# Split operands for the state products of a state space layer, and three moved loads, in a two-layer encoder

## The chip, the cores and the metric

The kernel runs on one core of a Trainium2 chip. A core has five engines that work side by side, each with its own in-order queue: PE (the matrix engine), DVE (vector work), ACT (scalar functions, casts), POOL and SP. SP computes nothing here; it issues most DMA transfers. An engine's queue stalls as a whole when the instruction at its head waits for a semaphore. The metric is the device time of one launch in microseconds (us); lower is better.

## What is computed

The reference is an encoder of two layers over 512 tokens of width 1024, in float32. Each layer is a token mixer and then a gated channel mixer (up-projection, convolution of width 3, gelu, down-projection), with RMS norms before and after each. The first mixer is retention plus neighbourhood attention. The second is a state space layer in both directions, and its chunked scan is where most of the change lies:

```python
def step(h, inp):                     # one chunk of 128 tokens
    qq, kk, vv, aa = inp
    cs = jnp.cumsum(aa, axis=1)
    ...
    y_inter = jnp.einsum('bjgn,bghnp->bjghp', qq, h) * jnp.exp(cs)[..., None]
    tail = jnp.exp(cs[:, -1:] - cs)
    h_new = h * jnp.exp(cs[:, -1])[..., None, None] \
          + jnp.einsum('blgn,blghp->bghnp', kk, vv * tail[..., None])
    return h_new, y_intra + y_inter
```

The last `einsum` is the state product: 128 state channels by 512 inner channels of a group, summed over the 128 tokens of a chunk. There are 4 groups, 4 chunks and 2 directions; the state after the last chunk is not needed, so 3 products are made for each group and direction, 24 in all.

## The kernel before

Tokens lie in 4 chunks of 128. Weights arrive as tiles of 128 by 1024 (512 KB) in `wst`, a staging pool of 3 buffers. `Env.wunit` (L61) issues the load on SP and has `Env.split` (L83) make two operands of it: ACT casts the tile to the reduced type `R32` (`whi`, L86), DVE subtracts that from the original (`wlo`, L87). `Env.mm3` (L89) then takes three products of split operands, high by high, low by high and high by low (L91, L92, L93). All the large projections are made this way. The small products of the mixers take plain F32 operands, one `matmul` call each.

No order is written out for the engines. The program is written as a sequence, a scheduler places each instruction in its engine's queue by its own idea of when it can run, and `high_priority` (L70) lets the weight splits go ahead. A change in one place can so move its neighbours.

The parts of the program, in order of time, with the names that matter here:

- `trunk` (L943) loads the four token tiles of x on SP, with the first norm's gain (`bcast`, L78, a row of 4 KB copied to all 128 partitions) after the first of them and a weight tile after each of the others. `E.norm` (L132) squares a tile of x on ACT (L128), takes the root on POOL (L121) and scales on DVE (`xs`, L139); `E.turn` (L143) transposes it on PE (`pt`, L148) and splits it (`xh`, `xl`).
- `mixer0`, then the first `ffn` (L224).
- `mixer1` (L563), the state space layer. It goes through its 4 groups by a table of steps, `SLOTS` (L551). Step `s` calls `state` (L725) for both directions: DVE scales a chunk of the input (`xs`, L730), PE makes the product with `bt`, the transposed B of the group (`st`, L732), and DVE adds it to the decayed state before (L738, L740), or ACT copies it for the first chunk (L735). Step `i` reads the states (`pi`, L783). Step `h` makes the decays of a head with 8 small ACT instructions on `pb` (L762), a DVE copy (L764), an exponential into `e` (L766) and a product (L768); `e` comes from the pool `m1e` of 5 buffers. Step `p` uses them (`py`, L803).
- At the end of `mixer1`, the output projection of the last group; `out_tile` reloads a half row of x from DRAM after each use of its buffer (L869, `x<-xd`, 8 loads on SP).
- the second `ffn`. It begins with the splits of its first four weight tiles (`w0`, L251): two go to `whi` and `wlo`, two to free buffers of its own, `hh` and `hl`.

Of the kernel before, what the change touches and what calls it, by code (L numbers as in the profile page):

```python
# [7 lines left out]
F32 = mybir.dt.float32  # L8
# [18 lines left out]
class Env:  # L27
# [32 lines left out]

    def wunit(self, src, parts=None):  # L61


        nc = self.nc
        st = self.wst.tile([P, 1024], F32, name="wst")
        nc.sync.dma_start(st, src)
        halves = slice(0, 512), slice(512, 1024)
# [9 lines left out]

    def bcast(self, row):  # L78

        g = self.gain.tile([P, D], F32, name="gain")  # L80
        self.nc.sync.dma_start(g, row.partition_broadcast(P))
        return g
# [139 lines left out]

def ffn(E, w_up, cw, w_down, g_post_row, done):

    nc, tc = E.nc, E.tc
    with ExitStack() as ctx:
        hp = ctx.enter_context(tc.tile_pool(name="ffn_h", bufs=NF))
        cp = ctx.enter_context(tc.tile_pool(name="ffn_c", bufs=1))
        cwt = cp.tile([P, 2, NF, 4], F32, name="cwt")
        nc.sync.dma_start(cwt, cw)  # L230
        hs = []
# [18 lines left out]
        extra = lambda i=0: [hp.tile([P, S], R32, name=n) for n in ("hh", "hh", "hl", "hl")]  # L250
        w0 = [[E.wunit(w_up[s, f], extra() if 2 * f + s >= 2 else None) for s in range(2)] for f in range(2)]  # L251
        p0 = [[E.mm.tile([P, S], F32, name="mm") for s in range(2)] for f in range(2)]
# [309 lines left out]

def mixer1(E, w_dt, w_fm, cw, dtc, cols, mask, w_out, g_post_row, done):  # L563

# [6 lines left out]
    with ExitStack() as ctx:  # L571
# [100 lines left out]

        def to_tok(src, dst):
            pt = E.px.tile([P, NT, P], F32, name="pt", tag="px")
            for c in range(NT):
                nc.tensor.transpose(pt[:, c], src[:, c * C:(c + 1) * C], E.ident)  # L676
            nc.scalar.copy(dst, pt)

# [20 lines left out]
        def silus(o):  # L699
# [6 lines left out]
            for r, _, i in o["silu"]:  # L706
                o["t"][i] = r
                if i == 0:
                    o["bt"] = one.tile([P, NT, P], F32, name="bt")
                    to_tok(r, o["bt"])  # L710
                elif 2 <= i < 6:
                    if "x" not in o:
                        o["x"] = two.tile([P, NT, 512], F32, name="xt")
                    to_tok(r, o["x"][:, :, (i - 2) * P:(i - 1) * P])
            o["silu"] = []
# [9 lines left out]
        def state(o, dr, i):  # L725
# [3 lines left out]
            xs = E.tmp.tile([P, 512], F32, name="xs", tag="tmp")  # L729
            nc.vector.tensor_tensor(hv(xs), hv(o["x"][:, c]), rows(1, dr, g, c), op=ALU.mult)  # L730
            ps = E.px.tile([P, 512], F32, name="st", tag="px")
            nc.tensor.matmul(ps, o["bt"][:, c], xs, start=True, stop=True)  # L732
            ns = one.tile([P, 512], F32, name=f"state{dr}{i}")
# [158 lines left out]
        steps()  # L892
        three, ys, last = pool("m1e", 5), pool("m1y", 2), pool("m1f", 1)
        for _ in range(3):
# [33 lines left out]
        def fin(t, n, m):  # L928
# [3 lines left out]
        ws = [E.wunit(w_out[NG - 1, 0, 0]) + E.wunit(w_out[NG - 1, 0, 1]),  # L932
              E.wunit(w_out[NG - 1, 1, 0], t4(one, ("state00", "state10", "state01", "state11"))) + E.wunit(w_out[NG - 1, 1, 1], t4(four, ("yh", "yh", "yl", "yl")))]
        first = [out_mm(gs[-1], 0, ws[n]) for n in range(2)]
        rms(gs[-1])
# [7 lines left out]
def trunk(tc, x, norms, ab, ssd, ffns, out):  # L943

    nc = tc.nc
    with ExitStack() as ctx:
        E = Env(ctx, tc)
        w0 = []
        for t in range(NT):
            nc.sync.dma_start(E.x[:, t, :], x[t * P:(t + 1) * P])  # L950
            if t == 0:
                g0 = E.bcast(norms[0, 0])
            else:
                w0.append(E.wunit(ab[0][0, len(w0)]))
# [20 lines left out]
        ffn(E, *ffns[0], norms[0, 3], then(norms[1, 0]))  # L975
        mixer1(E, *ssd, norms[1, 1], then(norms[1, 2]))
        ffn(E, *ffns[1], norms[1, 3], store)
        while E.late:
# [108 lines left out]
```

## Time and profile before

| | us |
|---|---|
| median of 3 runs (1420.84 to 1422.39) | 1422.07 |
| the profiled execution, its own time | 1422.91 |
| its span, first to last instruction | 1421.1 |
| PE busy | 1395.8 (98%) |
| DVE busy | 909.3 (64%) |
| ACT busy | 710.6 (50%) |
| start to the first transposition on PE | 8.17 |
| `mixer1` from its first state step to its last | about 700 to 1026 |

Busy times of PE are modelled and overlap from one matmul to the next, so they don't say alone how near PE is to its limit; the distance from one matmul's start to the next does. The profile's clock is the share of the full PE clock that was granted. Times on the axis count from the start of the span.

### The profile page before, as it was taken

The page shows a single profiled execution, that of the slowest core. Times are in us where ns is not written, and L with a number is a line of the kernel's source. Part 1 is how long each engine was busy: PE and PEld are TensorE (multiplying, and loading weights), DVE is VectorE, ACT ScalarE, POOL GpSimd, SP SyncE. Part 2 cuts the span into 40 slices and gives each one's busy share as a digit, 9 for nine tenths or more (in the row PEclk, how much of TensorE's full clock was granted, in tenths as well). Part 3 has the DMA queues.
Part 4 walks back from the last instruction along what each step waited for, and adds up shares of the span by engine and source line. Part 5 has one row for each costly group of instructions (what it writes and reads, how often), then busy time and mean ns, then how long its engine had stood idle before and what let it go on. Part 6 is the DMA issues. An engine that isn't in the chain of part 4 may idle for free.

```text
span 1421.1 us, 17833 instructions
## 1 busy us (share of the span) xinstructions
PE 1395.8 (98%) x6838; PEld 1141.2 (80%) x6838; DVE 909.3 (64%) x1345; ACT 710.6 (50%) x1194; POOL 60.9 (4%) x66
## 2 busy tenths in 40 slices
PE   7999999999999999999999999999989999999998
PEld 6877777898888888888788788787878888888886
DVE  7368888765656652347878686997785665664232
ACT  5346666444444432324878787487344444443230
POOL 1010110100000000000000000010110000000000
PEclk9999999999999999999999999999999999999999
DMA  7443232233233322323566464363342233333231
GB/s 284 150 132 104 85 89 80 77 108 104 89 104 91 102 89 93 129 106 106 140 183 182 148 184 143 101 190 112 124 144 74 91 102 91 102 96 98 89 104 60
DMA packets 56437, 166.33 MB, mean 117 GB/s; under 512 B 6689, under 2 KB 7457, under 8 KB 56353
## 3 DMA queue, kind: packets, MB, share of 16 engines
q1 hardware_dynamic: 48464, 149.99, 33.2%
q10 hardware_dynamic: 7888, 15.21, 3.9%
q8 instruction: 54, 0.88, 0.3%
q14 instruction: 31, 0.25, 0.1%
HBM read 157.57 MB, written 5.51 MB: 115 GB/s over the span
## 4 chain that ended last, share of the span: by engine, by line
PE 89%; DVE 4%; ACT 3%; issue 2%; DMA 1%; POOL 0%; DVEq 0%; SPq 0%; POOLq 0%; ACTq 0%
PE mm L91 27%; PE mm L92 27%; PE mm L93 27%; PE pi L783 2%; PE py L803 1%; PE st L732 1%; PE y L459 1%; PE pt L148 1%; PE sc L443 1%; DVE wlo L87 1%; PE pt L676 0%; PE sc L444 0%; ACT whi L86 0%; DMA x<-in_x 0%; PE pt L511 0%
## 5 line engine op out<-in xcount | busy, mean ns | idle before, releaser
L91 PE MATMUL mm<-xh,whi 128*128 128x512 f32 (+1 forms) x1216 | 463.9, 382 | 0.4 <-ACT xh L86 0.2
L93 PE MATMUL mm<-xl,whi 128*128 128x512 f32 (+2 forms) x1216 | 463.3, 381 | 0.0
L92 PE MATMUL mm<-xh,wlo 128*128 128x512 f32 (+2 forms) x1216 | 462.1, 380 | 0.0
L87 DVE TENSOR_TENSOR wlo<-wst,whi 128x1024 fp32r<-128x1024 f32 (+1 forms) x208 | 254.8, 1226 | 135.0 <-ACT whi L86 131.7
L86 ACT CAST whi<-wst 128x1024 fp32r<-128x1024 f32 (+1 forms) x208 | 216.5, 1042 | 145.1 <-PE mm L92 123.4
L91 PEld LDWEIGHTS mm<-xh,whi 128*128 128x128 f32 x1216 | 228.3, 188 | 45.7 <-issue 2.3
L93 PEld LDWEIGHTS mm<-xl,whi 128*128 128x128 f32 (+1 forms) x1216 | 228.1, 188 | 44.1 <-issue 1.1
L92 PEld LDWEIGHTS mm<-xh,wlo 128*128 128x128 f32 (+1 forms) x1216 | 228.4, 188 | 42.4 <-issue 0.2
L237 DVE SCALAR_TENSOR_TENSOR cv<-mm,cwt,cv 128x511 f32<-128x511 f32 x88 | 66.0, 750 | 150.5 <-ACT cv L236 150.5
L236 ACT ACTIVATE cv<-mm,cwt 128x512 f32<-128x512 f32 x88 | 68.7, 780 | 128.0 <-PE mm L93 128.0
L91 PE MATMUL mm<-whi,hh 128*128 128x512 f32 x288 | 112.0, 389 | 0.0
L92 PE MATMUL mm<-whi,hl 128*128 128x512 f32 x288 | 112.0, 389 | 0.0
L93 PE MATMUL mm<-wlo,hh 128*128 128x512 f32 x288 | 112.0, 389 | 0.0
L762 ACT ACTIVATE pb<-pb,tok 128x128 f32<-128x128 f32 x256 | 81.3, 391 | 5.7 <-DMA pb<-pd 3.2
L86 ACT CAST hh<-cv 128x512 fp32r<-128x512 f32 x44 | 27.3, 621 | 103.3 <-DVE cv L245 103.3
L238 DVE SCALAR_TENSOR_TENSOR cv<-mm,cwt,cv 128x511 f32<-128x511 f32 x88 | 66.0, 750 | 3.0
L93 PEld LDWEIGHTS mm<-wlo,hh 128*128 128x128 f32 x288 | 54.1, 188 | 11.3
L91 PEld LDWEIGHTS mm<-whi,hh 128*128 128x128 f32 x288 | 54.1, 188 | 11.2
L92 PEld LDWEIGHTS mm<-whi,hl 128*128 128x128 f32 x288 | 54.1, 188 | 11.2
L696 DVE SCALAR_TENSOR_TENSOR xf<-mm,cwt,xf 128x511 f32<-128x511 f32 (+1 forms) x64 | 47.5, 744 | 8.1 <-ACT xf L693 7.8
L87 DVE TENSOR_TENSOR hl<-cv,hh 128x512 fp32r<-128x512 f32 x44 | 30.5, 693 | 28.9 <-ACT hh L86 28.9
L128 ACT ACTIVATE junk<-mm 128x512 bf16<-128x512 f32 x24 | 14.3, 596 | 68.7 <-PE mm L93 68.6
(250 smaller groups left out, 1877.1 us busy)
## 6 DMA issues: line engine op xcount, KB each, us to landing
wst<-in_f_up SPq DMA_DIRECT2D x88, 512.0 KB
wst<-in_f_down SPq DMA_DIRECT2D x44, 512.0 KB
wst<-in_c_fm SPq DMA_DIRECT2D x40, 512.0 KB
pb<-pd ACTq DMA_DIRECT2D x29, 512.0 KB
wst<-in_ab_fm SPq DMA_DIRECT2D x20, 512.0 KB
gain<-yd SPq DMA_DIRECT2D x32, 256.0 KB
wst<-in_c_out SPq DMA_DIRECT2D x16, 512.0 KB
gain<-in_norms SPq DMA_DIRECT2D x8, 512.0 KB
```

The costliest lines, as they stand in the source:

```text
L86: self.nc.scalar.copy(hi, src)
L87: self.nc.vector.tensor_tensor(lo, src, hi.bitcast(F32), op=ALU.subtract)
L91: mm(out, lh, rh, start=first, stop=False)
L92: mm(out, ll, rh, start=False, stop=False)
L93: mm(out, lh, rl, start=False, stop=last)
L128: self.nc.scalar.activation(self.junk[:, :w], src, AF.Square, scale=float(n) ** -0.5, accum_out=s)
L236: nc.scalar.activation(o, ps, AF.Identity, scale=w(1), bias=w(3))
L237: nc.vector.scalar_tensor_tensor(o[:, 1:], ps[:, :S - 1], w(0), o[:, 1:], op0=ALU.mult, op1=ALU.add)
L238: nc.vector.scalar_tensor_tensor(o[:, :S - 1], ps[:, 1:], w(2), o[:, :S - 1], op0=ALU.mult, op1=ALU.add)
L696: nc.vector.scalar_tensor_tensor(r[:, a], ps[:, b], wc(j), r[:, a], op0=ALU.mult, op1=ALU.add)
L762: nc.scalar.activation(pb[:, dr, c], pb[:, dr, c], AF.Identity, scale=1.0 - 2 * dr, bias=tok[:, 0, c, dr * H + h:dr * H + h + 1])
L783: nc.tensor.matmul(pi[:, c - 1 + dr], o["st"][dr, i][:, q * P:(q + 1) * P], o["t"][1][:, c * C:(c + 1) * C], start=True, stop=True)
```

## The change

It has four parts.

1. In `mixer1`, both operands of the state product are split. `bt` becomes `bth` and `btl` (ACT casts from PSUM where it copied before, DVE subtracts), `xs` is split to `xsh` and `xsl` (a cast on ACT and a subtraction on DVE, both new), and `mm3` takes three products for the one plain product. The scaled input, its two halves and other small tiles share the pool `tmp` of 7 buffers. The pool of `e` has 4 buffers, not 5.
2. The first two weight tiles of the second `ffn` are loaded and split, and its third is loaded, before the output products of the last group are written (`ahead`). `ffn` takes them over.
3. The load of the first gain is issued by ACT, not by SP, and ACT then squares a single column, so that the table for its first function is loaded ahead of x.
4. In `ffn`, the load of the convolution's weights is written after those of the first weight tiles.

```diff
-    def wunit(self, src, parts=None):
-        nc = self.nc
+    def wload(self, src):
         st = self.wst.tile([P, 1024], F32, name="wst")
-        nc.sync.dma_start(st, src)
+        self.nc.sync.dma_start(st, src)
+        return st
+
+    def wunit(self, src, parts=None, st=None):
+        if st is None:
+            st = self.wload(src)
...
-    def bcast(self, row):
+    def bcast(self, row, eng=None):
         g = self.gain.tile([P, D], F32, name="gain")
-        self.nc.sync.dma_start(g, row.partition_broadcast(P))
+        (eng or self.nc.sync).dma_start(g, row.partition_broadcast(P))
...
-def ffn(E, w_up, cw, w_down, g_post_row, done):
+def ffn(E, w_up, cw, w_down, g_post_row, done, w1=None):
...
-        nc.sync.dma_start(cwt, cw)
...
-        w0 = [[E.wunit(w_up[s, f], extra() if 2 * f + s >= 2 else None) for s in range(2)] for f in range(2)]
+        u0, u1, st = w1 or (E.wunit(w_up[0, 0]), E.wunit(w_up[1, 0]), None)
+        w0 = [[u0, u1], [E.wunit(w_up[0, 1], extra(), st), E.wunit(w_up[1, 1], extra())]]
+        nc.sync.dma_start(cwt, cw)
...
-        def to_tok(src, dst):
+        def to_tok(src):
...
-            nc.scalar.copy(dst, pt)
+            return pt
...
-                    o["bt"] = one.tile([P, NT, P], F32, name="bt")
-                    to_tok(r, o["bt"])
+                    o["bt"] = [one.tile([P, NT, P], R32, name=n) for n in ("bth", "btl")]
+                    E.split(*o["bt"], to_tok(r))
...
-                    to_tok(r, o["x"][:, :, (i - 2) * P:(i - 1) * P])
+                    nc.scalar.copy(o["x"][:, :, (i - 2) * P:(i - 1) * P], to_tok(r))
...
             nc.vector.tensor_tensor(hv(xs), hv(o["x"][:, c]), rows(1, dr, g, c), op=ALU.mult)
+            xh, xl = (E.tmp.tile([P, 512], R32, name=n, tag="tmp") for n in ("xsh", "xsl"))
+            E.split(xh, xl, xs)
             ps = E.px.tile([P, 512], F32, name="st", tag="px")
-            nc.tensor.matmul(ps, o["bt"][:, c], xs, start=True, stop=True)
+            E.mm3(ps, o["bt"][0][:, c], o["bt"][1][:, c], xh, xl, True, True)
...
-        three, ys, last = pool("m1e", 5), pool("m1y", 2), pool("m1f", 1)
+        three, ys, last = pool("m1e", 4), pool("m1y", 2), pool("m1f", 1)
...
+        ahead()
         first = [out_mm(gs[-1], 0, ws[n]) for n in range(2)]
...
-                g0 = E.bcast(norms[0, 0])
+                g0 = E.bcast(norms[0, 0], nc.scalar)
+
+                nc.scalar.activation(E.junk[:, :1], E.mhalf, AF.Square)
...
-        mixer1(E, *ssd, norms[1, 1], then(norms[1, 2]))
-        ffn(E, *ffns[1], norms[1, 3], store)
+        w1 = []
+
+        def ahead():
+            up = ffns[1][0]
+            w1.extend((E.wunit(up[0, 0]), E.wunit(up[1, 0]), E.wload(up[0, 1])))
+
+        mixer1(E, *ssd, norms[1, 1], then(norms[1, 2]), ahead)
+        ffn(E, *ffns[1], norms[1, 3], store, w1)
```

The queues differ from those of before in the first hundred or so rows of PE and in `mixer1`; the last 1780 matmuls, the last 277 rows of DVE and the last 199 of ACT stand in the same order. Three places follow. The lines of the changed kernel are some 6 to 19 higher (its `mm3` is L97, L98, L99, its splits L92 and L93).

**First, the states of group 0.** PE before, in the middle of a projection (`mm`) of the same group: six state products in a row, then the first products that read states.

```order
L93 MATMUL mm<-xl,whi 128x512
L732 MATMUL st<-xs,bt 128x512 x6
L783 MATMUL pi<-cf,state_5655 128x128
L783 MATMUL pi<-cf,state_5667 128x128
L91 MATMUL mm<-xh,whi 128x512
```

PE after, the first state and the beginning of the second, with the projection's products between:

```order
L97 MATMUL st<-xsh,bth 128x512
L98 MATMUL st<-xsh,btl 128x512
L97 MATMUL mm<-xh,whi 128x512
L99 MATMUL st<-xsl,bth 128x512
L98 MATMUL mm<-xh,wlo 128x512
L99 MATMUL mm<-xl,whi 128x512
L97 MATMUL mm<-xh,whi 128x512
L98 MATMUL mm<-xh,wlo 128x512
L99 MATMUL mm<-xl,whi 128x512
L97 MATMUL mm<-xh,whi 128x512
L98 MATMUL mm<-xh,wlo 128x512
L97 MATMUL st<-xsh,bth 128x512
```

ACT after, at the same place: the new casts `xsh` stand among the small instructions of two heads (`pb`) and the copies of the first states.

```order
L92 CAST xsh<-xs 128x512
L772 ACTIVATE pb<-pb,tok 128x128 x5
L745 COPY state_5664<-st 128x512
L92 CAST xsh<-xs 128x512
L772 ACTIVATE pb<-pb,tok 128x128 x5
L745 COPY state_5676<-st 128x512
L92 CAST xsh<-xs 128x512
L776 ACT_TABLE_LOAD
L776 ACTIVATE e<-pb 128x512
L92 CAST xsh<-xs 128x512
```

The block of six has become six groups of three, eight products of the projection apart, and each waits for one more ACT and one more DVE instruction than before.

**Second, the start, on DVE.** `xs_130` and `xs_132` are the halves of the first token tile, `xs_152` and `xs_154` of the second; `wlo_109` is the low half of the first weight tile. Before:

```order
L139 SCALAR_TENSOR_TENSOR xs_130<-x_97,r_x_128,gain_103 128x512
L139 SCALAR_TENSOR_TENSOR xs_132<-x_97,r_x_128,gain_103 128x512
L139 SCALAR_TENSOR_TENSOR xs_152<-x_97,r_x_150,gain_103 128x512
L87 TENSOR_TENSOR wlo_109<-wst_106,whi_108 128x1024
L87 TENSOR_TENSOR xl_101<-pt_134,xh_100 128x4x128
L139 SCALAR_TENSOR_TENSOR xs_154<-x_97,r_x_150,gain_103 128x512
```

After (the numbers are one higher):

```order
L145 SCALAR_TENSOR_TENSOR xs_131<-x_97,r_x_129,gain_103 128x512
L93 TENSOR_TENSOR wlo_110<-wst_107,whi_109 128x1024
L145 SCALAR_TENSOR_TENSOR xs_133<-x_97,r_x_129,gain_103 128x512
L145 SCALAR_TENSOR_TENSOR xs_153<-x_97,r_x_151,gain_103 128x512
L93 TENSOR_TENSOR xl_101<-pt_135,xh_100 128x4x128
L93 TENSOR_TENSOR wlo_117<-wst_114,whi_116 128x1024
```

The low half of the first weight tile has moved ahead of two of the first three scalings of x.

**Third, the way into the second `ffn`.** SP before: the loads of the weight tiles (`in_f1_up`), two gains, and the reloads of x.

```order
L66 DMA wst_8911<-in_f1_up 128x1024
L81 DMA gain_8608<-in_norms 128x1024
L66 DMA wst_8917<-in_f1_up 128x1024
L66 DMA wst_8927<-in_f1_up 128x1024
L81 DMA gain_8696<-in_norms 128x1024
L66 DMA wst_8937<-in_f1_up 128x1024
L66 DMA wst_9195<-in_f1_up 128x1024
L869 DMA x_97<-xd_5142 128x512 x8
L66 DMA wst_9226<-in_f1_up 128x1024
```

SP after:

```order
L87 DMA gain_8761<-in_norms 128x1024
L64 DMA wst_8789<-in_c_out 128x1024
L64 DMA wst_8795<-in_f1_up 128x1024
L64 DMA wst_8801<-in_f1_up 128x1024
L64 DMA wst_8807<-in_f1_up 128x1024
L87 DMA gain_8863<-in_norms 128x1024
L64 DMA wst_9089<-in_f1_up 128x1024
L64 DMA wst_9348<-in_f1_up 128x1024
L879 DMA x_97<-xd_5143 128x512 x8
L64 DMA wst_9379<-in_f1_up 128x1024
```

ACT before, at the head of that `ffn`, where `hh` are the splits of the third and the fourth weight tile:

```order
L86 CAST xh_100<-pt_9002 128x4x128
L86 CAST whi_9228<-wst_9226 128x1024
L86 CAST hh_8923<-wst_8927 128x512
L86 CAST hh_8924<-wst_8927 128x512
L86 CAST hh_8933<-wst_8937 128x512
```

ACT after:

```order
L92 CAST xh_100<-pt_9155 128x4x128
L92 CAST whi_9381<-wst_9379 128x1024
L92 CAST hh_9077<-wst_8807 128x512
L92 CAST hh_9078<-wst_8807 128x512
L92 CAST hh_9085<-wst_9089 128x512
```

On SP one gain and one tile of the layer's own output weights have moved by a place or two; five of the `ffn`'s tiles were ahead of the reloads of x before, and five are now. On ACT the order is the same: the cast of the sixth tile, whose load stands behind the eight reloads, is ahead of the `hh` casts.

2 lines of the change are left out of this document (1 added, 1 removed).

## The prediction

> **What bounds the kernel now.** I read the page first, then the stretches of the stage that changes, then the rows of the operations themselves, and last the chain of work at the start and ahead of the second `ffn`.
>
> ```profile
> PE 1395.8 (98%) x6838; PEld 1141.2 (80%) x6838; DVE 909.3 (64%) x1345; ACT 710.6 (50%) x1194; POOL 60.9 (4%) x66
> ...
> PE 89%; DVE 4%; ACT 3%; issue 2%; DMA 1%; POOL 0%; DVEq 0%; SPq 0%; POOLq 0%; ACTq 0%
> ```
>
> The second line is the chain that ended last: 89% of the span is PE. Busy PE is not yet PE at its peak, so I look at how fast matmuls follow each other, in a stretch of the second `ffn` that holds only products of 128x512 in the reduced type, and in the state space layer's stage.
>
> ```profile
> core 0: us, PE busy (x) PEld busy (x) DVE busy (x) ACT busy (x) POOL busy (x), PEclk, DMA share, GB/s
> 1110.00:1190.00 80.00, 80.00 (x355) 66.24 (x354) 48.58 (x60) 34.51 (x44) 0.00 (x0) 1.00 0.31 97
> 700.00:1026.00 326.00, 323.72 (x1718) 260.54 (x1716) 259.82 (x384) 233.98 (x476) 19.81 (x14) 1.00 0.53 156
> ```
>
> 355 products in 80 us are 0.225 us each. In the layer's 326 us PE is busy for 323.7, with DVE at 80% and ACT at 72%. What PE waited for there is short:
>
> ```profile
> PE pss L830 <- POOL sq L815: 1.5, 2, 0.8
> PE pi L783 <- DVE state L740: 0.5, 1, 0.5
> PE mm L91 <- ACT hh L86: 3.9, 2, 3.2
> ```
>
> The first two rows are from that stage, the third from the way into the second `ffn`, the one long wait of PE behind the start. So **PE's own work sets the end**, and the change is worth what it takes off PE, less what its new ACT and DVE work makes PE wait.
>
> **The state products on PE.** Rows of the chain in group 1, and the group of all of them:
>
> ```profile
> 793.75 3.44 PE st L732 x8
> 797.19 0.89 PE pi L783 x8
> ...
> L732 PE MATMUL st<-xs,bt x48: 590/592/697, 703.5 to 974.7; 128*128 128x512 f32 x48
> ```
>
> The 24 plain products are 48 matmuls: one product in F32 is carried out as two, and eight take 3.44 us, 0.43 each. 48 x 0.43 = 20.6 us. After, there are 24 x 3 = 72 matmuls of the same shape as a projection's, at 0.225: 16.2 us. I take **-4.4 us**. The bounds are narrow, as both shapes are in the trace.
>
> **What the split adds beside PE.** Each state gets a cast and a subtraction of 128x512, for which the `ffn` has rows; the split of `bt` adds a subtraction for each group (its cast takes the place of a copy).
>
> ```profile
> L86 ACT CAST hh<-cv 128x512 fp32r<-128x512 f32 x44 | 27.3, 621 | 103.3 <-DVE cv L245 103.3
> L87 DVE TENSOR_TENSOR hl<-cv,hh 128x512 fp32r<-128x512 f32 x44 | 30.5, 693 | 28.9 <-ACT hh L86 28.9
> ```
>
> ACT: 24 x 0.62 = 14.9 us. DVE: 28 x 0.69 = 19.4 us. Over the 326 us ACT goes from 234 to 249 and DVE from 260 to 279, 76% and 86%: on the whole both fit beside PE. Where the states are, less so. These are 16 us of each group:
>
> ```profile
> 700.00:716.00 16.00, 15.39 (x71) 10.49 (x70) 13.64 (x22) 13.08 (x33) 0.00 (x0) 1.00 0.86 221
> 787.00:803.00 16.00, 16.00 (x86) 12.10 (x85) 13.44 (x24) 12.21 (x28) 0.00 (x0) 1.00 0.30 107
> 894.00:910.00 16.00, 16.00 (x64) 11.47 (x62) 15.26 (x24) 4.84 (x6) 0.00 (x0) 1.00 0.22 66
> 965.00:981.00 16.00, 16.00 (x72) 11.32 (x71) 14.74 (x24) 11.54 (x31) 0.00 (x0) 1.00 0.06 18
> ```
>
> DVE is busy for 57.1 of these 64 us; 19.4 more would be 76.5, **12.4 us too much** if PE needed it all there. That is the upper bound of the new waits. What speaks against it is the new order: the block of six products (six times 0.86, 5.2 us) is drawn out. From one state to the next stand its three products and eight of a projection, 11 x 0.225 = 2.5 us, while DVE has about four instructions (a scaling, a subtraction, two on the states before, each near 0.68 us as the first row below has it) = 2.7 us, and ACT a cast, a copy and five on `pb`:
>
> ```profile
> L730 DVE TENSOR_TENSOR xs<-xt,tok x24: 680/684/694, 702.6 to 973.4; 128x512 f32<-128x512 f32 x24
> ...
> 704.30 1.57 ACT L762 ACTIVATE pb<-pb,tok 128x128 f32<-128x128 f32 x5
> 705.77 0.56 ACT L735 COPY state<-st 128x512 f32<-128x512 f32 x1
> ```
>
> 1.57 + 0.56 + 0.62 = 2.75 us. So all three engines are within 0.3 us of each other, and the loop through a state (cast, product, copy) crosses engines, so I expect some 0.2 us at one state in three: 8 x 0.2 = 1.6 us. Against this, the waits that the block of six had itself go: PE's 0.5 us at `pi` above, and the steps between the last state product and what follows. In the rows above a state's second product lasts 0.59 us and the next starts 0.43 us after it, and the first `pi` behind such a block begins late by up to the difference of 0.16; four blocks give 0.6, together with the 0.5 some 1.1. Net **+0.5 us**; the lower bound is -1.1 (no new wait), the upper +12.4. I stay near the lower end because the projection's products stand between the states and DVE has its idle time right behind (in the whole stage 66 us).
>
> The three halves a state in `tmp` and the smaller pool of `e` are covered by the same order: a write to them waits for an earlier reader. The nearest row is this wait of ACT in the stage:
>
> ```profile
> ACT e L766 <- PE py L803: 3.6, 2, 3.4
> ```
>
> That is 3.6 us in two waits. ACT's `pb` and DVE's work on the heads are queued behind it. I cost one buffer less at nothing; the end is within the +12.4.
>
> **The start.** The gain is taken out of SP's queue.
>
> ```profile
> 2.00:4.20 2.20, 0.00 (x0) 0.00 (x0) 0.00 (x0) 0.00 (x0) 0.00 (x0) 1.00 0.98 302
> 4.20:6.50 2.30, 0.00 (x0) 0.00 (x0) 0.00 (x0) 2.24 (x2) 0.00 (x0) 1.00 0.96 285
> 6.50:7.80 1.30, 0.00 (x0) 0.00 (x0) 0.44 (x1) 0.19 (x2) 0.55 (x1) 1.00 1.03 422
> ...
> 4.25 1.28 ACT L128 ACT_TABLE_LOAD   x1 [4.25 <-DMA x<-in_x]
> ...
> 7.36 1.41 DVE L139 SCALAR_TENSOR_TENSOR xs<-x,r_x,gain 128x512 f32<-128x512 f32 x2 [5.96 <-POOL r_x L121]
> ...
> 9.06 1.04 ACT L86 CAST whi<-wst 128x1024 fp32r<-128x1024 f32 x1
> ...
> 9.67 0.75 DVE L139 SCALAR_TENSOR_TENSOR xs<-x,r_x,gain 128x512 f32<-128x512 f32 x1 [0.90 <-POOL r_x L121]
> ...
> 10.34 1.22 DVE wlo L87
> ```
>
> The first tile of x is there at 4.25, then ACT loads its table for 1.28 us. Between 4.20 and 6.50 the gain is under way, with the DMA engines busy for 96% of the time. The first weight tile, fourth in the row, is there at 9.06. The table load goes out of the way: the lower bound is -1.3 us. But with the DMA engines busy for 98%, 96% and 103% of these three stretches, I see no room that a second queue could fill; the first tile of x then shares them with the gain and may come as late as 6.5. And in the new order DVE's `wlo` of the first weight tile, which can't start before 9.06 + 1.04 = 10.1, holds up the second scaling of x, which was over by 8.8. At 10.34 DVE had three scalings done; now one, a lag of two, 1.4 us less the 0.2 by which `wlo` starts sooner: 1.2 us. PE has other products to fill in from about 14 us, so half of it may be taken up. I take **+0.6**, bounds -1.3 and +2.3 (the lag, and 1.1 us on ACT, whose first cast of x now stands behind the squares of the third tile).
>
> The Trainium skill (DMA: Bandwidth & Descriptors, Issuing engines are not separate DMA queues) says that transfers issued from different engines run on the same 16 DMA engines and interleave, and that only issue time is saved. It speaks against this edit, and the full DMA engines between 2.0 and 7.8 agree; without such a rule the term would be -1.3.
>
> **The way into the second `ffn`.** Chain and stretches:
>
> ```profile
> 1049.64 4.13 DMA wst<-in_f_up
> 1053.80 0.25 ACT whi L86
> ...
> 1054.75 1.66 ACT hh L86 x3
> ...
> 1052.20:1055.40 3.20, 0.01 (x1) 0.00 (x0) 2.82 (x5) 2.19 (x4) 0.35 (x1) 1.00 0.74 243
> 1055.40:1062.10 6.70, 6.03 (x26) 5.59 (x27) 4.75 (x7) 2.58 (x5) 1.08 (x1) 0.53 0.66 213
> ```
>
> PE stands still for 3.2 us, and for the next 6.7 us it is granted 0.53 of its clock, which costs about 6.7 x 0.47 = 3.1 us more. It waits for `hh`, whose loads were issued ahead of the reloads of x: ACT is held by the cast ahead of it, of the sixth weight tile, issued at 1049.64 behind the eight reloads of x. The change loads the third tile sooner, but the sixth is still behind the reloads and its cast is still ahead of `hh`. So I take **0**, with -3.2 - 3.1 = -6.3 as lower bound. The later load of the convolution's weights stands at the same place in SP's queue: 0.
>
> **Sum.** -4.4 + 0.5 + 0.6 + 0 = -3.3 us, on the profiled execution's own 1422.91: 1419.6. That execution was 0.8 us above the median of the runs shown, so I forecast **1418.8** for the median, 0.23% less.
>
> **Rivals.**
>
> - *The new waits are hidden* (no net term for them, or the gain of 1.1 at the blocks): 1418.3 down to 1417.2. For it: the projection's products between the states. Against: ACT's 2.75 us a state.
> - *The way into the `ffn` gets shorter.* If `hh` is free as its tile lands, the 6.3 us go: 1412.5. Against: the two orders on ACT. A part of it can come by itself: without the slow clock the time is 3.1 less, 1415.7. The Trainium skill (TensorE: Matmul & The Clock Gate, What's actually happening) has the clock halved after an idle window of some 3.4 us, in windows that run freely; by that rule an idle time of 3.2 us might halve it in one program and not in the next. The three runs before lie within 1.6 us, so there it did not come and go.
> - *DVE becomes the bound at the states, and the kernel is slower.* The 12.4 us don't fit, and PE, once out of projections to put between, waits for `xsl`: -4.4 + 12.4 + 0.6 = +8.6, 1430.7. It decides from new waits of 4.4 + 2.8 - 0.6 = 6.6 us, 0.28 us a state.
> - *The products don't get cheaper*, as three passes with three weight loads may take as long as two: each load in the window above is hidden (66 of 80 us), so 0.225 should hold. If not, -4.4 is 0 and the time 1423.2.
>
> **How the numbers follow.** A measurement of this kernel can tell about 0.2%, 2.8 us, from no change; faster means below 1419.2. My forecast with its small waits has a chance of 0.53, by itself between 1417 and 1421.5, and I put 0.25 of it below 1419.2; hidden waits 0.19, all faster; the shorter way into the `ffn` 0.12, faster; DVE as the bound 0.11, slower; products no cheaper 0.05, no difference. Faster 0.25 + 0.19 + 0.12 = 0.56, slower 0.11, same 0.28 + 0.05 = 0.33. The range leaves out DVE as the bound and the lowest part of the shorter way: 1413.5 to 1423.5.
>
> **What would show it.** The new products at 0.225 us from one to the next, and 72 of them; PE waits for `xsh` or `xsl` of 1 to 3 us in sum; DVE near 280 us in the stage; the first projection product on PE no sooner than before; the first tile of x landing later than 4.25; a wait of PE for `hh` of about 3 us and a granted clock near 0.5 behind it. The forecast is wrong if that wait is gone, if the sum of PE's waits for the states is over 6 us, or if the start has moved by more than 2 us.

## The result, and the profile after

The changed kernel takes 1444.52 us (median of 4 runs, 1436.75 to 1446.12) against 1421.45 for the kernel before beside it (4 runs, 1420.83 to 1422.39). The ratio is 1.0144, with a 95% interval of 1.0125 to 1.0164: **slower by 23.1 us**. The prediction had 1418.8, with a range from 1413.5 to 1423.5. One execution of all in this document, of the kernel called `no_casts_subs` below, was in a slow state, at 1994 us and 0.655 of the clock, and isn't counted.

The profiled execution took 1446.12 us, the longest of the four. The page's lines on the span, on busy time by engine and on the chain that ended last:

```profile
span 1444.3 us, 17915 instructions
...
PE 1402.5 (97%) x6862; PEld 1150.3 (80%) x6862; DVE 929.1 (64%) x1373; ACT 724.5 (50%) x1219; POOL 62.9 (4%) x66
...
PE 85%; DVE 6%; ACT 4%; DMA 3%; issue 2%; POOL 1%; SPq 0%; DVEq 0%; POOLq 0%; ACTq 0%
```

PE's idle time is the span less its busy time: 1421.1 - 1395.8 = 25.3 us before, 1444.3 - 1402.5 = 41.8 after. So 16.5 us of the 23.2 that the span grew are new idle time of PE. The other 6.7 are busy time, although 4.4 us of matmul work went. What PE waited for, from the head of the list of its waits (sum, times, longest); the first row is the start's and was 9.1 before, and `hh` was 3.9:

```profile
PE pt L154 <- DVE xs L145: 9.2, 3, 8.8
PE pt L684 <- ACT bf L710: 6.1, 1, 6.1
PE mm L97 <- ACT hh L92: 3.6, 2, 3.1
PE mm L97 <- ACT xh L92: 3.1, 3, 1.9
...
PE py L813 <- DVE e L778: 2.0, 2, 1.6
PE mm L97 <- ACT z L710: 1.8, 1, 1.8
PE sc L451 <- DVE rk L385: 1.6, 1, 1.6
...
PE st L97 <- ACT xsh L92: 0.9, 2, 0.7
```

The new products (`st`) hardly wait: 0.9 us for `xsh`, and `xsl` is not in the list (the weight loads of the third product, a list of their own, waited 0.9 us for it). The long waits are elsewhere, each for ACT or DVE at some other tile. Where the lost busy time is, the stretches show (us, PE busy, ..., then the granted clock):

```profile
720.00:722.00 2.00, 0.99 (x5) 0.46 (x3) 2.00 (x4) 1.98 (x4) 0.00 (x0) 1.00 0.47 184
722.00:724.00 2.00, 1.17 (x3) 0.99 (x4) 1.49 (x3) 1.99 (x5) 0.00 (x0) 0.75 0.08 30
724.00:726.00 2.00, 2.00 (x7) 1.63 (x7) 0.01 (x1) 1.98 (x3) 0.00 (x0) 0.50 0.00 0
726.00:728.00 2.00, 2.00 (x15) 1.87 (x14) 1.77 (x4) 1.84 (x6) 0.00 (x0) 0.90 0.05 16
...
944.00:948.00 4.00, 0.71 (x4) 0.24 (x2) 3.14 (x4) 1.69 (x5) 0.00 (x0) 1.00 0.64 193
948.00:951.00 3.00, 0.16 (x1) 0.17 (x2) 0.63 (x1) 2.97 (x7) 0.00 (x0) 0.54 0.70 259
951.00:954.00 3.00, 3.00 (x21) 2.34 (x22) 1.39 (x3) 2.75 (x6) 0.00 (x0) 0.50 0.10 38
954.00:957.00 3.00, 3.00 (x11) 2.46 (x12) 3.00 (x5) 3.00 (x12) 0.00 (x0) 0.82 0.00 0
```

Behind these two stops PE's clock is granted at half for 3 to 7 us, so each is paid for twice. For the first: 1.84 us idle in the first two rows and then 0.25 x 2 + 0.5 x 2 + 0.1 x 2 = 1.7 us of lost clock.

The longest new stop, at 944, can be followed back through three queues. First ACT, then DVE, then SP, each in its own timeline (start, duration, instruction, idle time before it and what ended it):

```profile
906.42 1.05 ACT L92 CAST whi<-wst 128x1024 fp32r<-128x1024 f32 x1
...
941.70 1.05 ACT L92 CAST whi<-wst 128x1024 fp32r<-128x1024 f32 x1 [6.24 <-DMA wst<-in_c_fm]
...
946.33 1.04 ACT L92 CAST whi<-wst 128x1024 fp32r<-128x1024 f32 x1 [2.31 <-DMA wst<-in_c_fm]
947.28 1.57 ACT L772 ACTIVATE pb<-pb,tok 128x128 f32<-128x128 f32 x5
948.86 1.28 ACT L710 ACT_TABLE_LOAD   x1
950.15 0.63 ACT L710 ACTIVATE bf<-bf 128x512 f32<-128x512 f32 x1
```

```profile
931.51 1.22 DVE L93 TENSOR_TENSOR wlo<-wst,whi 128x1024 fp32r<-128x1024 f32 x1
...
933.58 1.40 DVE L93 TENSOR_TENSOR wlo<-wst,whi 128x1024 fp32r<-128x1024 f32 x1
```

```profile
926.23 3.15 SPq L785 DMA_DIRECT2D gain<-yd  x4
932.80 0.33 SPq L64 DMA_DIRECT2D wst<-in_c_fm  x1
933.70 1.03 SPq L785 DMA_DIRECT2D gain<-yd  x1
935.07 0.33 SPq L64 DMA_DIRECT2D wst<-in_c_fm  x1
```

The load that the second cast waits for, in the chain that ended last; and, of SP's own waits in the layer, the row of the `gain` loads (in the step `i` the buffer `gain` holds a row of decays, which DVE's `ti` reads):

```profile
935.07 11.18 DMA wst<-in_c_fm
946.33 1.04 ACT whi L92
```

```profile
SPq L785 <- DVE ti L797: 52.8, 9, 20.7
```

PE needs `bf`, whose last activation is at 950.15 on ACT. ACT is held twice, at 941.70 and 946.33, by casts whose weight tiles land late. Their loads were issued at 932.80 and 935.07, each as soon as a subtraction on DVE (931.51 and 933.58) had given its staging buffer back. DVE runs both late: the cast at 906.42, done at 907.47, has its subtraction at 931.51, 24 us behind. DVE isn't waiting in between (it is idle for 0.6 us of the 24): 39 other instructions stand ahead of that subtraction in its queue. So DVE's queue is late, and what it holds up is a buffer that a DMA needs, which ACT needs, which PE needs.

But the buffer is only the last of what held these loads. In SP's queue four loads of `gain` stand ahead of them, and the first of those waited 20.7 us, to 926.23, for DVE's `ti`, which comes behind the states. With every subtraction in time the load of 932.80 could in this order have gone out at 929.4 at the soonest, 3.4 us earlier. And it then takes 8.9 us to land, the next one 11.2, behind the `gain` loads and loads of `pb`, where the weight load of 905.60 took 3.5.

### The profile page after: what moved, and what is told of

It is laid out like the page before. It is cut to its first block, busy times and chain, and to the rows that moved or that the text cites. A ratio compares the mean times of both kernels' runs of the same rounds, so it can differ in the third digit from the quotient of the medians.

```text
span 1444.3 us, 17915 instructions
## 1 busy us (share of the span) xinstructions
PE 1402.5 (97%) x6862; PEld 1150.3 (80%) x6862; DVE 929.1 (64%) x1373; ACT 724.5 (50%) x1219; POOL 62.9 (4%) x66
## 4 chain that ended last, share of the span: by engine, by line
PE 85%; DVE 6%; ACT 4%; DMA 3%; issue 2%; POOL 1%; SPq 0%; DVEq 0%; POOLq 0%; ACTq 0%
PE mm L97 26%; PE mm L98 25%; PE mm L99 25%; DMA pb<-pd 1%; PE pi L793 1%; PE py L813 1%; PE y L467 1%; DVE wlo L93 1%; PE pt L154 1%; DMA wst<-in_c_fm 1%; ACT whi L92 1%; DVE xf L704 1%; PE pt L684 1%; PE sc L451 1%; DMA x<-in_x 1%
## 5 line engine op out<-in xcount | busy, mean ns | idle before, releaser
L97 PE MATMUL mm<-xh,whi 128*128 128x512 f32 (+1 forms) x1216 | 465.2, 383 | 3.7 <-ACT z L710 1.8
L98 PE MATMUL mm<-xh,wlo 128*128 128x512 f32 (+2 forms) x1216 | 463.5, 381 | 0.8 <-DVE wlo L93 0.8
L99 PE MATMUL mm<-xl,whi 128*128 128x512 f32 (+2 forms) x1216 | 463.6, 382 | 0.0
L93 DVE TENSOR_TENSOR wlo<-wst,whi 128x1024 fp32r<-128x1024 f32 (+1 forms) x208 | 254.0, 1223 | 130.9 <-ACT whi L92 126.4
L92 ACT CAST whi<-wst 128x1024 fp32r<-128x1024 f32 (+1 forms) x208 | 216.6, 1042 | 144.9 <-PE mm L98 107.2
L97 PEld LDWEIGHTS mm<-xh,whi 128*128 128x128 f32 x1216 | 229.0, 188 | 49.8 <-ACT z L710 2.2
L98 PEld LDWEIGHTS mm<-xh,wlo 128*128 128x128 f32 (+1 forms) x1216 | 229.2, 188 | 43.8 <-DVE wlo L93 1.1
L99 PEld LDWEIGHTS mm<-xl,whi 128*128 128x128 f32 (+1 forms) x1216 | 228.8, 188 | 44.1 <-issue 0.8
L97 PE MATMUL mm<-whi,hh 128*128 128x512 f32 x288 | 112.0, 389 | 0.0
L98 PE MATMUL mm<-whi,hl 128*128 128x512 f32 x288 | 112.0, 389 | 0.0
L99 PE MATMUL mm<-wlo,hh 128*128 128x512 f32 x288 | 112.0, 389 | 0.0
L92 ACT CAST hh<-cv 128x512 fp32r<-128x512 f32 x44 | 27.3, 621 | 103.4 <-DVE cv L251 103.4
L97 PEld LDWEIGHTS mm<-whi,hh 128*128 128x128 f32 x288 | 54.1, 188 | 11.3
L98 PEld LDWEIGHTS mm<-whi,hl 128*128 128x128 f32 x288 | 54.1, 188 | 11.3
L99 PEld LDWEIGHTS mm<-wlo,hh 128*128 128x128 f32 x288 | 54.1, 188 | 11.1
L93 DVE TENSOR_TENSOR hl<-cv,hh 128x512 fp32r<-128x512 f32 x44 | 30.5, 693 | 28.9 <-ACT hh L92 28.8
```

Source lines behind the costliest of these rows:

```text
L92: self.nc.scalar.copy(hi, src)
L93: self.nc.vector.tensor_tensor(lo, src, hi.bitcast(F32), op=ALU.subtract)
L97: mm(out, lh, rh, start=first, stop=False)
L98: mm(out, ll, rh, start=False, stop=False)
L99: mm(out, lh, rl, start=False, stop=last)
```

## The experiments

All kernels were timed in five rounds beside the kernel before, whose median was 1421.8 to 1422.3 in every group of runs. I first took the change apart. The theory was that DVE and ACT work of the split and the order it makes had cost some 20 us and the start some 4; the rival was the smaller pool of `e`.

**The start alone.**

```
...
-                g0 = E.bcast(norms[0, 0])
+                g0 = E.bcast(norms[0, 0], nc.scalar)
+                nc.scalar.activation(E.junk[:, :1], E.mhalf, AF.Square)
```

> The kernel before with the start alone changed: the gain is loaded from ACT's queue and an activation stands ahead to load ACT's table. Theory of the start: the gain takes its share of the DMA engines from the first tile of x all the same, DVE's work on the first weight tile stands ahead of the second tile's scaling, and the later order of SP's queue in the first mixer changes with it; the trace after lay 1.3 us behind by 43 us and 3.9 behind by 110, so 1424.5 to 1426 us here. Rival: the 3.9 us are not the start's but come with the other two parts, through a shared order; then 1420.5 to 1422.

1424.55 us (11 runs, 1422.92 to 1426.54), ratio 1.0020, interval 1.0011 to 1.0029: **+2.7**. ACT's and DVE's timelines:

```profile
1.17 1.28 ACT L954 ACT_TABLE_LOAD   x1 [1.17 <-PEq L1079]
...
6.25 1.06 ACT L128 ACTIVATE junk<-x 128x1025 bf16<-128x1025 f32 x1 [3.57 <-DMA x<-in_x]
```

```profile
8.06 0.75 DVE L139 SCALAR_TENSOR_TENSOR xs<-x,r_x,gain 128x512 f32<-128x512 f32 x1 [6.66 <-POOL r_x L121]
9.91 1.22 DVE L87 TENSOR_TENSOR wlo<-wst,whi 128x1024 fp32r<-128x1024 f32 x1 [1.09 <-ACT whi L86]
11.05 1.41 DVE L139 SCALAR_TENSOR_TENSOR xs<-x,r_x,gain 128x512 f32<-128x512 f32 x2
```

The table load is out of the way, and the first tile of x comes at 6.25 where it came at 4.25, now that the gain's load is issued beside it; the first transposition on PE starts at 8.87 instead of 8.17. DVE's second scaling starts at 11.05 behind the first `wlo`. Both are as the prediction had them. How long PE is busy in the first 20 us, the sums of the stretches tell, of `start_only` and then of before:

```profile
sum 20.00, PE 9.31 PEld 7.62 DVE 10.52 ACT 11.40 POOL 3.39; mean PE 1.86 PEld 1.52 DVE 2.10 ACT 2.28 POOL 0.68
```

```profile
sum 20.00, PE 11.30 PEld 8.95 DVE 11.46 ACT 11.24 POOL 3.14; mean PE 2.26 PEld 1.79 DVE 2.29 ACT 2.25 POOL 0.63
```

PE has done 2.0 us less, and by then no other product has filled the lag in.

**The buffer of `e` alone.**

```
-        three, ys, last = pool("m1e", 5), pool("m1y", 2), pool("m1f", 1)
+        three, ys, last = pool("m1e", 4), pool("m1y", 2), pool("m1f", 1)
```

> The kernel before with the pool of e, pb and m at four buffers instead of five, nothing else. Theory of the buffer: ACT's exponentials wait for PE's readers of e, the heads behind them on ACT come late, and that is most of the 20 us which the trace after lost between 700 and 1060 us; then 1433 to 1441 us. Rival, that the 20 us come from the split's own work and from the order that it makes: 1421 to 1424 us.

1428.84 us (5 runs, 1425.21 to 1430.09), ratio 1.0041, interval 1.0028 to 1.0053: **+7.0**, between the two. PE's waits and ACT's timeline show where:

```profile
PE py L803 <- DVE e L768: 2.8, 1, 2.8
```

```profile
807.96 0.62 ACT L766 ACTIVATE e<-pb 128x512 f32<-128x512 f32 x1
...
815.64 1.87 ACT L762 ACTIVATE pb<-pb,tok 128x128 f32<-128x128 f32 x6 [3.46 <-DMA pb<-pd]
...
821.03 1.14 ACT L766 ACTIVATE e<-pb 128x512 f32<-128x512 f32 x2
```

With five buffers the second exponential is at 808.94 (in the trace of before); with four the next two stand together at 821.03, behind activations that had to wait for a load of `pb`, and PE waits 2.8 us for `e`. So what shows here is less a wait for a buffer than another order of ACT's queue, which comes with the smaller pool. This profile was 4.1 us above the one of before, so the median's 7.0 is not all in it.

**The split alone, and the loads ahead alone.** The first is the change's edit of `state`, `silus` and `to_tok` with four buffers of `e` (five have no room beside it), the second is `ahead`, `wload` and the new `w1` of `ffn`.

> The kernel before with the states' products alone split (the smaller pool of e is needed for the room). All theories of the state space layer have the loss of about 20 us here, 1439 to 1444 us; the rival is that part of it is the third piece's, the loads ahead for the next ffn, which stand in the same queue: then 1421 to 1430 us.

> The kernel before with the next ffn's first weights alone loaded ahead of the reloads of x. By the trace after, where PE's stop at the way into the ffn was as long as before (3.2 us) and 0.8 us came back behind it: 1420.5 to 1422 us. Rival, that the stop would go if the layer ahead ran in its old order: 1415 to 1418 us.

`split_only` 1439.03 us (5 runs, 1435.93 to 1443.72), ratio 1.0118, interval 1.0098 to 1.0138: **+17.2**, 10.2 above `e4_only`. `ahead_only` 1421.49 us (11 runs), ratio 0.9997, interval 0.9988 to 1.0006: **no difference**, with PE's wait for `hh` where it was (3.7 us in two waits, the longest 3.1).

So the split costs 10.2 us beyond the buffer, though its products should give 4.4 back. Two theories: ACT, whose casts stand in order among the heads' activations; and DVE, whose subtractions fill it up. Four kernels tell them apart, all with four buffers of `e`.

```
no_casts_subs: scaling writes xh (reduced type);     mm3(ps, bth, btl, xh, xh)
casts_alone:   scaling xs, cast xh on ACT;           mm3(ps, bth, btl, xh, xh)
subs_alone:    scaling writes xh; xl = x - xh (DVE); mm3(ps, bth, btl, xh, xl)
split_first:   with tc.high_priority(100): E.split(xh, xl, xs)
```

> split_only without the casts and subtractions of xs: DVE's scaling writes the high half itself, in the reduced type, and the third product reads that high half again, so the low half of xs is left out of the states. PE's three products, the split of bt and the four buffers of e stay. If the loss is in the work that the split puts on ACT and DVE (by either engine), the products' 4.4 us show: e4_only's 1428.8 less 4.4, 1424 to 1428 us. Rival, that the three passes themselves or the smaller pool hold PE up: 1434 us or more.

> split_only with the casts of xs on ACT and without the subtractions on DVE: the third product reads the high half again, so the low half of xs is left out. Theory of ACT's queue (the casts stand in order among the heads' activations, so a state takes 2.5 us, the inter-chunk products come late, and with them the loads on SP that wait for their readers): the loss stays, 1433 to 1440 us. Theory of DVE (its subtractions fill it up): 1424 to 1430 us.

> split_only with the subtractions on DVE and without the casts on ACT: DVE's scaling writes the high half itself, and the subtraction takes it from the unscaled x, so the low half holds other numbers. Theory of ACT's queue: most of the loss goes, 1424 to 1430 us. Theory of DVE: it stays, 1433 to 1440 us.

> split_only with the same work and another order: the cast and the subtraction of xs are put ahead of the heads' activations by priority. Theory of ACT's queue: what is lost by waiting behind those activations comes back, 1427 to 1434 us. Theory of DVE, whose work is the same: 1436 to 1442 us.

1425.10 (10 runs), 1426.10 (12 runs), 1435.12 (5 runs) and 1434.39 us (5 runs). Without the new work beside PE the time is 3.7 us under `e4_only`: **the products' gain is there**. ACT's casts add 1.0, too little to tell from nothing here. **DVE's subtractions add 10.0** (`subs_alone` over `no_casts_subs`) **to 12.9** (`split_only` over `casts_alone`). The theory of ACT's queue falls. Order counts as well: the same work with the split ahead is 4.6 us faster.

If DVE is short of time, another engine for the subtractions should mend it. And with five buffers of `e`, in room gained by cutting unused columns, the split might beat the kernel before.

```
...
-            E.split(xh, xl, xs)
+            nc.scalar.copy(xh, xs)
+            nc.gpsimd.tensor_tensor(xl, xs, xh.bitcast(F32), op=ALU.subtract)
```

> split_only with the 24 subtractions of the states on POOL instead of DVE, nothing left out. If it is DVE's time that is short, taking 24 subtractions off it gives what casts_alone gave (1426.1), though POOL takes 1.5 us for a 128x512 where DVE takes 0.69: 1424 to 1430 us. Rival, that the time from a scaling to its third product counts and not DVE's load: POOL's longer step makes it no better than split_only, 1436 to 1442 us.

> The kernel before with unused room taken out (padding columns and the end of the scratch of the squares), so that five buffers of e fit beside the split; a control for the next two. No work changes: 1420.5 to 1423 us. If addresses matter, it is off by more than 2 us, and the next two are read against it.

> The split with five buffers of e, in the room of before_trim. If the buffer's loss (7.0 us by e4_only) and DVE's add up: 1439.0 less 7.0, 1430 to 1434 us. If DVE's lag covers the wait for the buffer, or the order changes with it: 1436 to 1441 us.

> Five buffers of e and the subtractions on POOL together, nothing left out. If these two are the whole loss of the split, the products' 4.4 us are left as a gain against before: 1416.5 to 1420 us. If ACT's casts and POOL's longer step still cost, 1420 to 1424; if the loss is elsewhere, 1430 or more.

`subs_pool` 1443.78 us (4 runs), **worse** than `split_only`. Its groups by line, PE's waits, and the same group in `split_only`:

```profile
L730 DVE TENSOR_TENSOR xs<-xt,tok 128x512 f32<-128x512 f32 x24 | 27.8, 1163 | 7.8 <-ACT xt L714 7.8
```

```profile
PE st L93 <- POOL xsl L733: 10.7, 18, 1.1
```

```profile
L730 DVE TENSOR_TENSOR xs<-xt,tok 128x512 f32<-128x512 f32 x24 | 16.5, 686 | 5.6 <-ACT xt L714 5.6
```

Now PE does wait at the states, 18 times, and DVE's scalings take 1163 ns instead of 686 while POOL works beside them. So this run takes nothing off the way to the third product and doesn't decide between DVE's load and that way. `before_trim` is 1425.17 (12 runs, 1423.27 to 1428.58), +2.9 although no work changed and the queues of PE, DVE and ACT stand in the same order, so the control itself is off; its profile, the slowest of the 12, has a wait of 2.1 us for `rk` in the first mixer that before has at 0.2 (and after at 1.6, in the list above). `split_e5` is 1437.34 (6 runs) and `subs_pool_e5` 1448.93 (4 runs). Against `split_only` the fifth buffer is worth 1.7 us, or 4.6 with the control's 2.9, but the runs' ranges overlap; against `subs_pool` the kernel with five is 5.2 us slower. What the buffer is worth beside the split stays open.

Load, or a longer way? Three kernels have one without the other; `no_start` asks whether the parts add up.

```
subs_unused:  E.split(xh, xl, xs);                 mm3(ps, bth, btl, xh, xh)
casts_twice:  copy(xh, xs); copy(xl, xh) on ACT;   mm3(ps, bth, btl, xh, xl)
load_only:    e4_only + xl = xs - x on DVE, unread; matmul(ps, bt, xs)
no_start:     the changed kernel, gain and table as before
```

> split_only with everything in place, but the third product reads the high half of xs again, so nothing waits for the subtractions and the low half of xs is left out of the states. DVE has all its work, the way from a scaling to its products is that of casts_alone. If DVE's load is what costs: 1435 to 1440 us, near split_only. If it is the length of the way through a state: 1425 to 1429 us, near casts_alone.

> split_only with a second copy on ACT in the place of DVE's subtraction: the way from a scaling to its third product is as long as in split_only (0.6 us for 0.69), DVE has none of the new work, and the low half of xs holds the high half. If DVE's load is what costs: 1426 to 1431 us. If it is the length of the way: 1434 to 1440 us.

> e4_only, with the plain products, and 24 subtractions of 128x512 on DVE, one behind each scaling, which nothing reads. If DVE's load is what costs, it costs here as well, without any split: 1428.8 plus some 10, 1436 to 1442 us. If not: 1428 to 1432 us.

> The changed kernel with its start undone: the split, four buffers of e and the loads ahead. If the parts add up, split_only's 1439.0 less 0.3: 1437.5 to 1440.5 us. If the loads ahead cost something beside the split that they don't cost alone, 1441 us or more, and the 2.7 of the start is less in the whole.

`subs_unused` 1427.34 (5 runs): DVE's whole load costs 1.2 us over `casts_alone` when nothing waits for it. `casts_twice` 1423.91 (11 runs): the longer way costs nothing when it goes through ACT; with the products' gain this is the best of the splits, 4.9 under `e4_only` and 15.1 under `split_only`. It is also 2.2 faster than `casts_alone`, which does less, so differences of a microsecond or two between these kernels are no prices of work. `load_only` 1433.63 (6 runs, two at 1427.30 and 1428.90, four from 1433.61 to 1435.12): 4.8 over `e4_only`. So **neither theory holds alone**: with the split, 10 to 15 us come only where the third product waits for a subtraction that stands in DVE's queue.

Each of these edits also changes the order that the scheduler writes. Row by row, the queues of `subs_unused` differ from those of `split_only` in some 100 of DVE's 1373 rows and 230 of PE's 6862. So the wait in itself and the order that comes with it are not told apart: no run has the order of `split_only` without the wait. `no_start` 1438.84 (4 runs): as `split_only`, with the same order on PE, DVE and ACT, so the loads ahead add nothing that these runs can tell. The start then takes 1444.5 - 1438.8 = 5.7 us in the whole where it took 2.7 alone; the two ranges (1436.75 to 1446.12, 1435.08 to 1440.98) don't settle the difference.

What do the runs that lose have in common? In the traces I paired each cast of a weight tile of 128x1024 on ACT with its subtraction on DVE, for subtractions from 690 to 1050 us, and took the time from the end of the one to the start of the other. PE's idle time is span less busy time, of the profiled execution.

| | median us | PE idle | PE busy | lag of `wlo`, mean | longest |
|---|---|---|---|---|---|
| before | 1421.45 | 25.3 | 1395.8 | 2.0 | 11.1 |
| casts_twice | 1423.91 | 28.0 | 1394.3 | 2.0 | 11.0 |
| casts_alone | 1426.10 | 29.6 | 1393.0 | 1.6 | 11.0 |
| subs_unused | 1427.34 | 30.4 | 1395.1 | 3.3 | 12.9 |
| e4_only | 1428.84 | 28.7 | 1396.5 | 1.9 | 11.1 |
| load_only | 1433.63 | 33.1 | 1399.8 | 3.6 | 23.7 |
| split_first | 1434.39 | 34.4 | 1396.9 | 4.1 | 24.0 |
| subs_alone | 1435.12 | 36.4 | 1396.8 | 4.0 | 24.1 |
| split_only | 1439.03 | 37.9 | 1399.4 | 4.2 | 24.1 |
| after | 1444.52 | 41.8 | 1402.5 | 4.3 | 24.0 |

The five slowest of the table all have that one subtraction 24 us behind its cast, and all have a stop of PE that begins between 933 and 945, at the `bf` of the last group. The lag is one of order more than of load: in `split_only` and in `load_only` 39 instructions of DVE stand between this cast and its subtraction, in `subs_unused`, with as much work on DVE, 20, and in before, at the same place, 16. The last pair of runs makes it smaller; `self.wp` is 100 in the state space layer and 60 elsewhere:

```
             with self.tc.high_priority(60):
-                self.split(hi, lo, st)
+                self.nc.scalar.copy(hi, st)
+            with self.tc.high_priority(self.wp):
+                self.nc.vector.tensor_tensor(lo, st, hi.bitcast(F32), op=ALU.subtract)
```

> split_only with one thing moved: in the state space layer DVE's subtraction for a weight tile (wlo) is put further ahead of DVE's other work, by a priority of 100 in the place of 60. Theory of DVE's queue: what costs is that wlo comes up to 24 us behind its cast (at 926.6 in split_only; 11 in before), so that the staging buffer comes free late, the next load lands late, and ACT stands at its cast with the group's activations behind it; with wlo ahead PE's stop of 5 us at 939 and the slow clock behind it go, and the time is 1428 to 1433 us. Rival, that wlo's lag only goes along with the loss: 1436 to 1442 us.

> The kernel before with wlo put ahead in the same way, as a control. It has no stop of PE of this kind to lose: 1420 to 1424 us. If it gets faster by 3 us or more, the way is a gain of its own and says nothing on the split.

`before_wlo100` 1422.16 us, ratio 0.9999, interval 0.9990 to 1.0008. `split_wlo100` **1437.47 us** (4 runs, 1434.31 to 1441.20), ratio 1.0109, interval 1.0094 to 1.0125. The longest lag is 15.5 us and the mean 3.5, and the stop at `bf` is smaller, as the lists of waits of `split_wlo100` and of `split_only` show:

```profile
PE pt L678 <- ACT bf L704: 1.1, 1, 1.1
```

```profile
PE pt L676 <- ACT bf L702: 4.8, 1, 4.8
```

The time is not. The stop went as it should, PE's idle time in the profile fell from 37.9 to 1439.4 - 1405.9 = 33.5 us, and PE's busy time rose from 1399.4 to 1405.9, with a mean clock of 0.989 instead of 0.993; that profile was also the slowest of its four runs. So the lag of `wlo` goes with that one stop, and **is not the cause of the whole**: PE stops elsewhere instead (2.0 us at `pss`, 1.1 at `wo`). With the same matmuls set side by side, PE is 6.3 us ahead of `split_only` at 960 and 1.9 behind it by 1050. What is shown is that DVE's subtractions, where the third product waits for them, cost 10 to 15 us (10.0, 11.7, 12.9 and 15.1 in four pairs of kernels), together with the order that they bring; which of DVE's late results stops PE differs from order to order, and how the 10 to 15 divide stays open. None of the versions beats the kernel before.

## Why the prediction was wrong, step by step

**The state products** (-4.4) were right. There are 72, and they take what a projection's take. The chain that ended last, in group 2, and the row of the first of the three products, 24 of the 72:

```profile
908.54 0.23 PE st L98
...
909.25 0.23 PE st L99
```

```profile
L97 PE MATMUL st<-xsh,bth x24: 387/396/632, 708.5 to 1006.1; 128*128 128x512 f32 x24
```

From the start of one to that of the next it is 0.23 us (median), where the plain ones had 0.43. Where DVE gets no new work at the states the time fell by 3.7 (`no_casts_subs`), 2.7 (`casts_alone`) and 4.9 us (`casts_twice`). The rival by which they would be no cheaper falls.

**"Net +0.5 us" of new waits** is the step that failed. If the buffer's 7.0 below add to it, the runs have 10.2 + 4.4 = 14.6 us in its place, above its upper bound of 12.4. That the two are so near is in part luck: the bound was DVE's overtime in the windows of the states, and with that same overtime `subs_unused` lost 1.2 us and `load_only` 4.8. The choice near its lower end was wrong. It rested on "the projection's products stand between the states and DVE has its idle time right behind", and the first half of this is so: PE doesn't wait at the states (0.9 us). But DVE comes out of them late, and behind the states its queue holds work that others need soon: `ti`, which SP's next loads wait for, the subtractions of the weights, whose staging buffers SP needs as well, and the products of the heads. Of the signs that I set for being wrong, over 6 us of waits for the states did not come, and the wait for `hh` did not go; the start did move by more than 2 us, which is a small part of the loss. I looked for the price at the new instruction and not at what is queued behind it. The rival with DVE as the bound (0.11) had the engine and nearly the price right, and its place, PE waiting for `xsl`, wrong.

DVE's busy time was forecast well: 278.9 us in the layer's 345 us, against some 280. An engine at 81% of a stage ran one instruction 24 us after its operands were there, since 39 others stood ahead of it in the queue.

**"I cost one buffer less at nothing"** also failed: 7.0 us alone. The row that the prediction quoted for it, ACT's wait for `py` of 3.6 us in two waits, hardly grew, to 4.0. What grew is ACT's wait for loads of `pb`, from 3.2 to 10.2 us: the "ACT's `pb` and DVE's work on the heads" that the prediction named beside the row and put at nothing.

**The start** (+0.6) had the mechanism right and the size wrong: the first tile of x at 6.25 and the second scaling of x behind `wlo`, as described, but +2.7, above its bound of +2.3. "PE has other products to fill in ... so half of it may be taken up" is the part that failed, and the first tile's own lateness, 0.7 us at the first transposition, had no term. The Trainium skill (DMA: Bandwidth & Descriptors, Issuing engines are not separate DMA queues) spoke against this edit, and these rows agree with it.

**The way into the second `ffn`** (0) was right: -0.3 alone, within what can be measured. The wait for `hh` is 3.1 us, as before, and the clock behind it is again near half:

```profile
1079.50:1086.00 6.50, 5.99 (x30) 5.40 (x31) 4.74 (x7) 2.46 (x5) 1.19 (x1) 0.59 0.59 202
```

**No term at all** stood for the clock behind new stops. In after busy time grew by 6.7 us while 4.4 us of work went, so slower matmuls cost about 11 us, two thirds as much again as the 16.5 us of new idle time. The mean clock of the two profiles, 0.990 and 0.996, gives some 9.

The parts measured alone sum to 2.7 + 17.2 - 0.3 = 19.6 of the 23.1 us. The other 3.5 lie within the ranges of the runs, and were not traced further.

## What to carry over

Work given to an engine that is not the bound is paid for by what stands behind it in that engine's queue: list what that is, and who needs it (buffers to be given back to a DMA above all), before calling it hidden. Where a window's sum says that an engine is over its time, give that price a fair chance if a product of the bounding engine waits for the new instruction: here it cost 10 to 15 us with such a wait and 1 to 5 without. An edit that changes the order of the queues is an experiment on the order too; compare the orders before naming a cause. A buffer taken away for room is a change of its own; measure it alone.

## What the runs showed of the hardware that I had not expected

**The clock falls after short stops, by where they lie.** In after, PE was idle for 1.84 us between 720 and 724 and had half its clock right behind (the rows above). In `e4_only` it was idle for 2.8 us and kept its clock:

```profile
821.00:824.00 3.00, 0.48 (x3) 0.06 (x1) 3.00 (x5) 1.59 (x4) 0.00 (x0) 1.00 0.68 200
824.00:826.00 2.00, 1.71 (x22) 1.57 (x23) 1.89 (x4) 1.43 (x3) 0.00 (x0) 1.00 0.91 248
```

The traces keep every change of the granted clock, and in all twenty the changes lie whole multiples of 3.41 us apart. Counted in windows of that length, the stop of 1.84 us in after lies in one (719.57 to 722.98), and the clock halves at its end. The stop of 2.8 us in `e4_only` is cut by the end of a window at 823.02 into 1.53 and 1.28 us, and the clock stays. Over the twenty traces, from 20 to 1405 us and without windows that were already at half, all 37 windows in which PE was idle for 1.9 us or more were followed by half the clock, and 3 of the 33 with 1.0 to 1.6 us: here some half of a window is enough.

The Trainium skill (TensorE: Matmul & The Clock Gate, What's actually happening) has the clock fall after an idle window of some 3.4 us, in windows that run freely. The windows agree with the traces; that all of one must be idle does not, as 1.84 us was enough, and here the traces decide.

**POOL slows DVE.** With 24 subtractions of 1.47 us on POOL, DVE's scalings took 1163 ns on average instead of 686: the 15 that overlap one of them 1451, the other 9 683. DVE's additions `state<-st,state`, which read PSUM as one input, took 680 beside POOL and 685 alone. The Trainium skill (GPSIMD Engine Reference, 1. Specifications) says that POOL shares its SBUF interfaces with DVE and contends with DVE's instructions that have two SBUF inputs, as this scaling has; the trace agrees. An engine that is 4% busy was no free place for the work.
